# Experts in turn from four groups, a matmul branch for experts of at most 32 tokens, and the adding back moved

## The chip, the cores and the metric

The kernel runs on one core of one Trainium2 chip. The metric is the device time of one execution in microseconds (us), as the median over runs. The four compute engines have queues of their own: PE multiplies matrices (its weight loads are shown as PEld), DVE and ACT work on vectors and empty PSUM, POOL does little here, and SP issues most of the DMA transfers.

## The reference

The reference is a network of one batch of 512 tokens with 1024 columns in float32: an attention layer and a gated convolution layer, each followed by a SwiGLU layer, and then a block with windowed attention, an mLSTM and a mixture of experts. Only the last part, `hier_moe`, is touched:

- A router picks for every token one of 4 groups, and in that group the two best of 8 experts; so there are 32 experts and 1024 choices.
- Every expert e computes `(silu(x @ w_gate[e]) * (x @ w_up[e])) @ w_down[e]` for its tokens, with gate and up of 1024 x 512 and down of 512 x 1024.
- The result is multiplied by the token's weight and added to the token's row.

With the reference's inputs the router gives the experts these numbers of tokens, counted by running the reference's router (experts 0 to 31, eight to a group): 65 46 63 47 45 47 78 67 | 26 9 30 13 26 46 32 22 | 18 33 22 32 9 48 26 10 | 20 17 20 27 15 15 14 36. So 20 experts have at most 32 tokens, and three have more than 64: experts 0, 6 and 7.

## The kernel before

The layers ahead of the experts stream their weights through PE as products of split parts (`mm3`, lines 127 to 131) and take the first 1660 us. They stay as they are. The experts follow in one loop over e from 0 to 31 (lines 1545 to 1576), with the last one written out behind it. PE's instructions keep the order in which they are written (`manual_schedule`).

The work of an expert is done on 64 slots, the first 64 of its tokens. `place` (L1298) gives each choice its place among the tokens of its expert; a one-hot matrix of tokens by slots gathers the columns of the tokens (`gather`, L1395, for four experts at a time). In the order of PE one turn of the loop is:

- `turned` (L1440, tile htp): the hidden rows of expert e - 1 are transposed; ACT copies them to hT (L1442).
- `hidden` (L1431 and L1432, tile gu): gate and up of expert e. For each of 8 blocks of 128 rows there are two matmuls with 64 slots as the stationary part and 512 columns of weights moving; up's outputs go to one half of the partitions, gate's to the other. After the fourth and the eighth block `add_back_four` (L1467, tile cmb) puts in four matmuls that bring the outputs of expert e - 2 back to the rows of the tokens, and DVE adds each to X (L1469).
- `down` (L1452, tile y): the products of expert e - 1 with its down weights, for 4 blocks of 128 hidden columns, the two halves of the output columns side by side. ACT and DVE split and weight the outputs (L1457, L1459).
- An If on `any2` (L1562): if expert e or e - 1 has more than 64 tokens, the second 64 slots are worked on in `late_hidden` and `late_out`. PE, ACT and DVE read the count and branch.
- `gather` of a part of the next group (L1395), and `slot_weights` (L1421, tile otp), which transposes the weighted one-hot matrix into oT for the adding back; DVE takes the slots' weights from it (L1423).

The weights come in 192 pieces of 1 MB, six to an expert: gate, up, gate, up (halves of the rows), down, down. A ring of 14 buffers holds them, and `load_pieces` (L1188) issues them on SP's queue in order of use, each when its buffer comes free. In turn e the six pieces up to number 6e + 17 are asked for: their buffers are the ones of gate and up of expert e and of down of expert e - 1, so they come free when the If of turn e is over.

PSUM tiles come from two rings of four banks: "g" holds gu and y, "m" holds cmb, gat, otp and htp in the order in which they are written.

Of the kernel before, what the change touches and what calls it, by code (L numbers as in the profile page):

```python
# [9 lines left out]
F32 = mybir.dt.float32  # L10
# [11 lines left out]
P = 128  # L22
T = 512
# [18 lines left out]
def blocks_kernel(ctx: ExitStack, tc: tile.TileContext, a, out):  # L42
# [71 lines left out]
    def weave(*streams):  # L114
        """Emit the parts of several streams evenly: each is (generator, number of its parts)."""
# [11 lines left out]
    def mm3(ps, ah, al, bh, bl, start, stop):  # L127
        """ps += (ah + al)^T (bh + bl)"""
# [4 lines left out]
    def rsqrt(dst, src, n, eps, scale=1.0):  # L133
        """dst = 1 / sqrt(scale * src + eps) over [P, n], by three steps of Newton's; each turns the sign"""
# [4 lines left out]
    def newton(dst, h, n):  # L139
        """dst = 1 / sqrt(2 h)"""  # L140
# [13 lines left out]
    # -------------------------------------------------------------- constants  # L154
# [5 lines left out]
    def load_xt(t):  # L160
        """a token tile of x, columns on partitions, where its rows go later"""
# [9 lines left out]
    def to_T_half(xt, src, t, g):  # L171
        """512 columns (half g) of token tile t into the transposed pair."""
# [10 lines left out]
    # per-channel vectors, channels on partitions  # L183
# [23 lines left out]
    # relative position bias of every offset, the largest first, from which rows that start one  # L207
    # element further from row to row give the Toeplitz tile of a head, its columns turned round
# [15 lines left out]
    class Norm:  # L224
        """X = layer_norm(ALPHA X + m), tile after tile; the residual also gives the sums of the rows"""
# [30 lines left out]
    def rms_half(t, hh, ss, scr):  # L256
        """half of the mean of the squares of 512 columns' share"""
# [3 lines left out]
    def rms_scale(ss, eps):  # L261
        """1 / rms of a token tile from the two shares of half the mean square"""
# [7 lines left out]
    def out_parts(nk):  # L270
        """k ranges of an output projection for each half of the columns"""
# [8 lines left out]
    def out_half0(kh, kl, nk, fin, first=None):  # L280
        """The first 512 columns of k^T w for all tokens, token-major, k chunk after k chunk."""
# [45 lines left out]
    def proj_tm(xt, *evacs):  # L327
        """The next chunks' 256 columns token-major: evac(t, psum [128 tokens, 256])."""
# [10 lines left out]
    # ================================================ layer 0: diff attention  # L339
# [23 lines left out]
    with tc.tile_pool(name="att", bufs=2, side="right", reuse_waits="tile") as ap_, \  # L363
# [5 lines left out]
        def rotary(x):  # L369
            """rotate the first 16 of every 64 columns of x [P, NT, 256]"""  # L370
# [45 lines left out]
        def head_scores(u):  # L416
            """softmax difference of one head and query tile; one reciprocal row sum is left out"""
# [67 lines left out]
            # token tiles of a head that are normed together after the last of them  # L485
# [68 lines left out]
    # =============================================================== swiglu  # L554
# [3 lines left out]
    def proj_T(xt, evac, nk=KD):  # L558
        """The next chunk's 256 columns as rows: evac(i, psum [128 columns, tokens])."""
# [9 lines left out]
    def proj_T_first(xt, *evacs):  # L569
        """The same for the next two chunks, the first half of the tokens before the second."""  # L570
# [50 lines left out]
    # ================================================= layer 1: gated conv  # L621
# [51 lines left out]
    # ==================================================== second block, norm 1  # L673
# [21 lines left out]
    # gate rows: forward ig 0-3, backward ig 32-35, forward fg 64-67, backward fg 96-99  # L695
# [30 lines left out]
    def norm1_gain():  # L726
        """the gain of norm 1, which the weights behind it take up"""
# [6 lines left out]
    # ------------------------------------------- windowed attention, mLSTM  # L734
# [26 lines left out]
    # both parts of the 64 channels of a head one below the other, and the other way round  # L761
# [4 lines left out]
    def head_norm(x, n):  # L766
        """x [P, NT, n * 64] over its rms per 64 columns"""
        v = x.rearrange("p t (h e) -> p t h e", e=64)
        ss = small.tile([P, NT, n], F32, tag="hss", name="hss", bufs=1)
# [5 lines left out]
        rs = small.tile([P, NT, n], F32, tag="hrs", name="hrs", bufs=1)  # L775
# [18 lines left out]
    def proj_qk_m():  # L794
        """conv and twice the silu of the mLSTM queries and keys, channels on partitions"""
# [35 lines left out]
    def window_attn():  # L831
# [20 lines left out]
        def queries(i):  # L852
            """the two parts of two heads"""
# [20 lines left out]
    def window_scores(u):  # L874
        """softmax numerators of two heads of one query tile"""
# [48 lines left out]
    def branch_T(y, scales=None):  # L924
        """token-major y [P, NT, 512] into the transposed pair yT"""
# [24 lines left out]
    def proj_o():  # L950
        """sigmoid of the output gate"""
# [173 lines left out]
    def merge(i, out_cb):  # L1125
        """twice sigmoid(mg + b) * (y w) for one branch, rows are output columns"""
# [20 lines left out]
    # ------------------------------------------------------ merge, output  # L1147
# [34 lines left out]
    def load_pieces(end):  # L1182
        """the pieces up to the given number, those of an expert after those of the one before"""
        for n in range(sum(len(got) for got in pieces.values()), min(end, 6 * E_)):
# [3 lines left out]
            nc.sync.dma_start(p, a[key][0, e][hh * rows * P:(hh + 1) * rows * P]  # L1188
# [8 lines left out]
    iota65 = rt.tile([P, SLOTS], F32, tag="iota65", name="iota65")  # L1197
    nc.gpsimd.iota(iota65, [[1, SLOTS]], base=SLOTS + 1, channel_multiplier=0, allow_small_or_imprecise_dtypes=True)
# [450 lines left out]
```

## Time and profile before

| | us |
|---|---|
| three runs | 2274.31, 2275.84, 2276.46 |
| median | 2275.84 |
| span of the profiled execution | 2276.5 |
| PE busy in the span | 2173.3 (95%) |
| first to last gate/up matmul of the experts, start | 1664.46 to 2254.4 |

The page gives no time of the profiled execution beside its span; the span lies 0.04 us above the longest of the three runs. Times in the rows are counted from the span's start. A row of the timeline tells when an instruction began, how long it was in flight, its engine and line, and in brackets how long the engine had been idle before it and what ended the idle time. Matmuls overlap: one that is in flight for 0.59 us may be followed by the next after 0.43 us, so PE's pace is read from starts.

### The profile page before, as it was taken

Reading aid. Unit: us, or ns where it says so; the run is one execution under the profiler, and the core shown is the slowest. Engines: PE = TensorE matmul, PEld = TensorE weight load, DVE = VectorE, ACT = ScalarE, POOL = GpSimd, SP = SyncE. Lnnn points to the kernel's source line nnn. Section 1 sums busy time; section 2 is a strip of 40 time slices with the busy share of each in tenths; the row PEclk is TensorE's granted clock in tenths of the full one; section 3 lists DMA queues with packets and bytes.
Section 4 is the critical chain, followed back from the end, with each engine's and each line's share of the span. In section 5 each row is a group of like instructions: output and inputs, shape, how many; then the busy total and the mean of one; then the engine's idle time right before and its main releaser. Section 6 shows DMA issues by size and latency. Waiting matters only on the chain. (4 is left out here: it accounts for less than half of the span.)

```text
span 2276.5 us, 28917 instructions
## 1 busy us (share of the span) xinstructions
PE 2173.3 (95%) x11411; PEld 1623.8 (71%) x11412; DVE 1210.0 (53%) x2535; ACT 748.8 (33%) x1452; POOL 103.5 (5%) x90
## 2 busy tenths in 40 slices
PE   7999999999999999999997899999989989999997
PEld 7998788888888888888887788788844434444432
DVE  3788743332274463333237985774536445555555
ACT  3667533222132233232125454443322121212121
POOL 1000000000000000000012212121000000000000
PEclk9999999999999999999998999999999999999998
DMA  6210242232323223222232211323558849999994
GB/s 209 72 61 20 75 130 93 94 106 78 111 93 109 95 93 110 94 93 93 88 98 79 74 45 49 84 75 106 210 185 320 321 161 337 391 383 388 386 385 161
DMA packets 205290, 350.24 MB, mean 154 GB/s; under 512 B 8180, under 2 KB 101610, under 8 KB 205120
## 3 DMA queue, kind: packets, MB, share of 16 engines
q1 hardware_dynamic: 200784, 335.80, 42.2%
q0 software_dynamic: 3760, 11.09, 1.6%
q8 instruction: 112, 1.84, 0.3%
q10 hardware_dynamic: 576, 1.05, 0.1%
q14 instruction: 58, 0.48, 0.1%
HBM read 345.77 MB, written 2.13 MB: 153 GB/s over the span
## 5 line engine op out<-in xcount | busy, mean ns | idle before, releaser
L65 DVE TENSOR_TENSOR wlo<-raw,whi 128x1024 fp32r<-128x1024 f32 (+1 forms) x266 | 319.1, 1222 | 447.4 <-ACT whi L64 446.4
L130 PE MATMUL pT<-xl,whi 128*128 128x512 f32 (+1 forms) x1184 | 442.9, 374 | 1.3 <-DVE xl L65 1.3
L131 PE MATMUL pT<-xh,whi 128*128 128x512 f32 (+1 forms) x1184 | 443.1, 374 | 0.0
L129 PE MATMUL pT<-xh,wlo 128*128 128x512 f32 (+1 forms) x1184 | 442.5, 374 | 0.0
L64 ACT ACTIVATE whi<-raw 128x1024 fp32r<-128x1024 f32 (+1 forms) x266 | 258.1, 1005 | 345.4 <-PE po L131 169.2
L1431 PE MATMUL gu<-piece,xg 128*64 128x512 f32 x560 | 255.9, 601 | 4.8 <-DVEq L1580 2.7
L1432 PE MATMUL gu<-piece,xg 128*64 128x512 f32 x560 | 255.9, 601 | 0.0
L1469 DVE TENSOR_TENSOR X<-X,cmb 128x512 f32<-128x512 f32 x280 | 173.3, 683 | 152.3 <-PE cmb L1467 152.0
L130 PEld LDWEIGHTS pT<-xl,whi 128*128 128x128 f32 x1184 | 224.0, 189 | 40.2 <-DVE xl L65 1.7
L131 PEld LDWEIGHTS pT<-xh,whi 128*128 128x128 f32 x1184 | 223.8, 189 | 38.8
L129 PEld LDWEIGHTS pT<-xh,wlo 128*128 128x128 f32 x1184 | 223.8, 189 | 38.1
L129 PE MATMUL pq<-whi,xl 128*128 128x256 f32 x608 | 180.2, 296 | 14.1 <-ACT whi L64 12.6
L130 PE MATMUL pq<-wlo,xh 128*128 128x256 f32 x608 | 176.7, 291 | 7.8 <-DVE wlo L65 7.8
L131 PE MATMUL pq<-whi,xh 128*128 128x256 f32 x608 | 176.9, 291 | 0.0
L1431 PEld LDWEIGHTS gu<-piece,xg 128*64 128x64 f32 x560 | 71.7, 137 | 142.8 <-issue 135.0
L131 PE MATMUL po<-whi,hh 128*128 128x512 f32 x352 | 140.4, 399 | 0.0
L129 PE MATMUL po<-whi,hl 128*128 128x512 f32 x352 | 140.1, 398 | 0.0
L130 PE MATMUL po<-wlo,hh 128*128 128x512 f32 x352 | 140.1, 398 | 0.0
L1452 PE MATMUL y<-piece,hT 128*64 128x512 f32 x560 | 129.2, 604 | 2.1 <-ACT hT L1442 2.1
L129 PEld LDWEIGHTS pq<-whi,xl 128*128 128x128 f32 x608 | 120.2, 198 | 14.8 <-ACT whi L64 12.5
L130 PEld LDWEIGHTS pq<-wlo,xh 128*128 128x128 f32 x608 | 120.1, 198 | 8.8 <-DVE wlo L65 8.5
L131 PEld LDWEIGHTS pq<-whi,xh 128*128 128x128 f32 x608 | 120.0, 197 | 0.2
(402 smaller groups left out, 3078.4 us busy)
## 6 DMA issues: line engine op xcount, KB each, us to landing
piece<-in_w_expert_gate SPq DMA_DIRECT2D x64, 1024.0 KB, 7.7
piece<-in_w_expert_up SPq DMA_DIRECT2D x64, 1024.0 KB, 10.2
piece<-in_w_expert_down SPq DMA_DIRECT2D x64, 1024.0 KB, 14.3
raw<-in_ffn_w_gate SPq DMA_DIRECT2D x22, 1024.0 KB, 5.3
raw<-in_ffn_w_up SPq DMA_DIRECT2D x22, 1024.0 KB, 5.3
raw<-in_ffn_w_down SPq DMA_DIRECT2D x20, 1024.0 KB, 5.0
raw<-in_w_in SPq DMA_DIRECT2D x19, 1024.0 KB, 5.1
raw<-in_conv_w_in SPq DMA_DIRECT2D x12, 1024.0 KB, 5.1
```

Of the source, the lines that this page charges most:

```text
L64: act.activation(hi, src, AF.Copy)
L65: dve.tensor_tensor(out=lo, in0=src, in1=hi.bitcast(F32), op=ALU.subtract)
L129: pe.matmul(ps, al, bh, start=start, stop=False)
L130: pe.matmul(ps, ah, bl, start=False, stop=False)
L131: pe.matmul(ps, ah, bh, start=False, stop=stop)
L1431: pe.matmul(gu[rows], xs(k), pc_[2 + k // 4][:, k % 4, :], **st)
L1432: pe.matmul(gu[other], xs(k), pc_[k // 4][:, k % 4, :], **st)
L1452: pe.matmul(y[rows], hT[:, f, :], pc_[4 + f // 2][:, f % 2, c * 512:(c + 1) * 512], **st)
L1469: dve.tensor_tensor(out=sl, in0=sl, in1=ps, op=ALU.add)
```

## The change

The experts are numbered anew: `ORDER` takes one from each group in turn, and the weights, the router's expert numbers (`iotae`) and the loop over the remaining blocks follow it. In the new order the numbers of tokens are, from turn 0 to turn 31: 65 26 18 20 46 9 33 17 63 30 22 20 47 13 32 27 45 26 9 15 47 46 48 15 78 32 26 14 67 22 10 36.

`cnt` now holds the number of tokens of each expert, and `hidden` and `down` each read it on PE alone and branch. For more than 32 tokens the matmuls are those of before. For at most 32 tokens gate and up are done as four tiles of 32 columns at once, each on 32 slots and 256 columns of weights, after one bf16 matmul of zeros that starts the bank; and down as four tiles, two for the halves of the output columns times two for the halves of the hidden rows. To make this work, slots 32 to 63 of such an expert get the same tokens as slots 0 to 31 (`io`, `few`), so that adding back sums the two halves of down. The adding back of expert e - 2 is no longer inside `hidden`: four of its matmuls come before `hidden(e)` and four after it; in the last turn all eight of expert 30 come behind `hidden(31)`.

```diff
+    ORDER = [8 * (n % G_) + n // G_ for n in range(E_)]
...
-            nc.sync.dma_start(p, a[key][0, e][hh * rows * P:(hh + 1) * rows * P]
+            nc.sync.dma_start(p, a[key][0, ORDER[e]][hh * rows * P:(hh + 1) * rows * P]
...
-    pc = psum.tile([1, E_], F32, tag="m", name="pc")
+    pcs_ = psum.tile([P, E_], F32, tag="m", name="pc")
...
+    dve.tensor_scalar(out=few, in0=pcs_, scalar1=float(HALF), scalar2=None, op0=ALU.is_le)
...
+        dve.scalar_tensor_tensor(out=io[:, HALF:], in0=few[:, e:e + 1].to_broadcast([P, HALF]), scalar=-float(HALF),
+                                 in1=iota1[:, HALF:], op0=ALU.mult, op1=ALU.add)
...
+    def gate_up_few(gu, xs, pc_):
+        zero = ident[0:HALF].bitcast(BF16)[:, 2 * HALF:].unsqueeze(1)
+        pe.matmul(gu, zero[:, :, 0:P], zero[:, :, 0:P].to_broadcast([HALF, 4, P]), start=True, stop=False)
+        for k in range(KD):
+            st = dict(start=False, stop=k == KD - 1)
+            for q in range(4):
+                cs = slice(q % 2 * 256, q % 2 * 256 + 256)
+                pe.matmul(gu[quarter(q), cs], xs(k)[:, 0:HALF],
+                          pc_[(2 if q < 2 else 0) + k // 4][:, k % 4, cs], **st)
+
+    def few_tokens(e):
+        return nc.values_load(cnt[0:1, e:e + 1], engines=[ET.PE], min_val=0, max_val=2 * T,
+                              skip_runtime_bounds_check_because="a count of choices") <= HALF
...
+        gu = pbank("g", "gu")
+        with tc.If(few_tokens(e)) as c:
+            gate_up_few(gu, xs, pieces[e])
+        with c.Else():
+            gate_up_all(gu, xs, pieces[e], LOW)
+        activated(gu, s, LOW)
...
+    def down_few(y, hT, pc_):
+        for f in range(2):
+            st = dict(start=f == 0, stop=f == 1)
+            for q in range(4):
+                c, i = divmod(q, 2)
+                pe.matmul(y[quarter(q)], hT[:, 2 * i + f, quarter(i)],
+                          pc_[4 + i][:, f, c * 512:(c + 1) * 512], **st)
...
+            if e > 1:
+                add_back_four(e - 2, 0)
...
-            hidden(lambda k: xg[:, k, r * SLOTS:(r + 1) * SLOTS], pieces[e], ss[e], LOW, between)
+            hidden(e, lambda k: xg[:, k, r * SLOTS:(r + 1) * SLOTS], ss[e])
+            if e > 1:
+                add_back_four(e - 2, 1)
             if e > 0:
-                ys[e - 1] = down(hT, pieces[e - 1], ws[e - 1], "y")
+                ys[e - 1] = outputs(down(e - 1, hT), ws[e - 1], "y")
...
+        hidden(e, lambda k: xg[:, k, r * SLOTS:(r + 1) * SLOTS], ss[e])
...
+        add_back_four(e - 1, 0)
+        add_back_four(e - 1, 1)
+        yy = outputs(down(e, turned(ss[e], LOW)), sw, "y")
```

Beside this, the late slots of an expert are found with another DVE operation of the same size, two small tiles of the windowed attention (`hss`, `hrs`) move to another pool, and comments go.

## Rows read from the trace of the kernel before

**Rows 1.** The page: busy time, clock and DMA rate in 40 slices of 56.9 us.

```profile
PE 2173.3 (95%) x11411; PEld 1623.8 (71%) x11412; DVE 1210.0 (53%) x2535; ACT 748.8 (33%) x1452; POOL 103.5 (5%) x90
...
PEclk9999999999999999999998999999999999999998
...
GB/s 209 72 61 20 75 130 93 94 106 78 111 93 109 95 93 110 94 93 93 88 98 79 74 45 49 84 75 106 210 185 320 321 161 337 391 383 388 386 385 161
```

**Rows 2.** Stretches: busy us of PE, PEld, DVE, ACT, POOL; clock, DMA share, GB/s.

```profile
1711.00:1879.00 168.00, 156.28 (x764) 70.51 (x764) 86.97 (x155) 34.26 (x61) 0.00 (x0) 0.99 0.73 270
1993.00:2205.00 212.00, 205.63 (x1026) 91.40 (x1026) 122.29 (x224) 42.83 (x78) 0.00 (x0) 1.00 1.03 386
```

**Rows 3.** Timeline of PE in one turn (expert 18).

```profile
2025.56 0.64 PE L1431 MATMUL gu<-piece,xg 128*64 128x512 f32 x1
2025.57 0.64 PE L1432 MATMUL gu<-piece,xg 128*64 128x512 f32 x1
2026.04 0.59 PE L1431 MATMUL gu<-piece,xg 128*64 128x512 f32 x1
...
2029.14 1.19 PE L1467 MATMUL cmb<-y,oT 128*128 128x512 f32 x4
...
2030.27 0.64 PE L1431 MATMUL gu<-piece,xg 128*64 128x512 f32 x1
...
2034.98 3.65 PE L1452 MATMUL y<-piece,hT 128*64 128x512 f32 x16
...
2039.09 0.36 PE L1395 MATMUL gat<-oh,h2l 128*128 128x256 f32 x1 [0.46 <-PEq L1562]
...
2041.93 0.64 PE L1431 MATMUL gu<-piece,xg 128*64 128x512 f32 x1
```

**Rows 4.** Timeline: the first gate/up matmul of experts 0, 2, 6, 9, 20, 31.

```profile
1664.46 0.64 PE L1431 MATMUL gu<-piece,xg 128*64 128x512 f32 x1
...
1713.94 0.64 PE L1431 MATMUL gu<-piece,xg 128*64 128x512 f32 x1
...
1779.41 0.64 PE L1431 MATMUL gu<-piece,xg 128*64 128x512 f32 x1
...
1878.12 0.64 PE L1431 MATMUL gu<-piece,xg 128*64 128x512 f32 x1
...
2058.29 0.64 PE L1431 MATMUL gu<-piece,xg 128*64 128x512 f32 x1
...
2244.94 0.81 PE L1431 MATMUL gu<-piece,xg 128*64 128x512 f32 x1 [2.71 <-DVEq L1580]
```

**Rows 5.** SP issues by tile up to the first 24 pieces, and the next issue.

```profile
piece<-in_w_expert_gate SPq DMA_DIRECT2D x8, 1024.0 KB, 5.9
...
1727.15 0.37 SPq L1188 DMA_DIRECT2D piece<-in_w_expert_gate  x1
```

**Rows 6.** One stretch, columns as in rows 2.

```profile
1723.00:1724.00 1.00, 1.00 (x6) 0.34 (x6) 1.00 (x3) 0.00 (x0) 0.00 (x0) 1.00 0.02 8
```

**Rows 7.** Timeline of DVE, the same turn.

```profile
2023.89 1.53 DVE L1459 SCALAR_TENSOR_TENSOR y<-y,sw 64x512 fp32r<-64x512 f32 x2
...
2025.96 0.69 DVE L1423 TENSOR_REDUCE sw<-otp 128x1 f32<-128x512 f32 x1 [0.53 <-ACT oT L1422]
```

**Rows 8.** Lines of the If and of its load: ns min/median/max, first and last start.

```profile
L1562 PEldq COMPARE_BRANCH  x31: 70/330/433, 1667.7 to 2230.0; - x31
...
L1508 PEldq TENSOR_LOAD <-any x31: 297/302/493, 1667.1 to 2229.6; - x31
```

**Rows 9.** Waits of PE: us in total, times, longest.

```profile
PE gat L1395 <- PEq L1562: 10.6, 23, 0.6
PE cmb L1467 <- DVE y L1459: 10.0, 7, 2.3
...
PE gat L1395 <- PEq L1566: 1.0, 1, 1.0
```

**Rows 10.** Timeline of DVE ahead of the first turn.

```profile
1665.71 0.16 DVE L1352 CAST cnt<-ex 1x32 int32<-1x32 f32 x1
```

More of the change, by code (lines that the diff above doesn't have):

```diff
@@ L1210, in blocks_kernel @@
     nc.gpsimd.iota(iota, [[1, SLOTS]], base=0, channel_multiplier=0, allow_small_or_imprecise_dtypes=True)
+    iotae = r1.tile([P, E_], F32, tag="iotae", name="iotae")
+    nc.gpsimd.iota(iotae, [[1, E_ // G_], [E_ // G_, G_]], base=0, channel_multiplier=0,
+                   allow_small_or_imprecise_dtypes=True)
     sel = r1.tile([P, NT, E_], BF16, tag="sel", name="sel")
@@ L1351, in blocks_kernel @@
         dve.scalar_tensor_tensor(out=ex, in0=pc, scalar=float(SLOTS * m), in1=ex, op0=ALU.is_gt, op1=ALU.add)
[L1352 to L1356 removed]
+    dve.tensor_copy(cnt, pc)
+    dve.tensor_copy(any2[:, 0:1], ex[:, 0:1])
+    dve.tensor_tensor(out=any2[:, 1:E_], in0=ex[:, 1:E_], in1=ex[:, 0:E_ - 1], op=ALU.add)
     ge = r1.tile([P, NT, G_], F32, tag="ge", name="ge")
@@ L1423, in slot_weights, with quarter, gate_up_all @@
         dve.reduce_max(out=w, in_=ps, axis=AX.X)
-    def hidden(xs, pc_, s, rows, between=lambda k: None):
-        gu = pbank("g", "gu")
+    def quarter(i):
+        return slice(i * HALF, (i + 1) * HALF)
+    def gate_up_all(gu, xs, pc_, rows):
         other = HIGH if rows == LOW else LOW
@@ L1432, in hidden, with activated @@
             pe.matmul(gu[other], xs(k), pc_[k // 4][:, k % 4, :], **st)
-            between(k)
+    def gate_up_few(gu, xs, pc_):
[10 more added lines that the diff above has]
+                              skip_runtime_bounds_check_because="a count of choices") <= HALF
+    def activated(gu, s, rows):
+        other = HIGH if rows == LOW else LOW
         act.activation(s[rows], gu[other], AF.Silu)
         dve.tensor_tensor(out=s[rows], in0=s[rows], in1=gu[rows], op=ALU.mult)
+    def hidden(e, xs, s):
+        gu = pbank("g", "gu")
[4 more added lines that the diff above has]
+        activated(gu, s, LOW)
     def turned(s, rows):
@@ L1452, in down, with outputs @@
                 pe.matmul(y[rows], hT[:, f, :], pc_[4 + f // 2][:, f % 2, c * 512:(c + 1) * 512], **st)
-        between()
+    def down_few(y, hT, pc_):
[5 more added lines that the diff above has]
+                          pc_[4 + i][:, f, c * 512:(c + 1) * 512], **st)
+    def down(e, hT):
+        y = pbank("g", "y")
+        with tc.If(few_tokens(e)) as c:
+            down_few(y, hT, pieces[e])
+        with c.Else():
+            down_all(y, hT, pieces[e])
+        return y
+    def outputs(y, w, tag):
         yt = x1.tile([P, 2, T], F32R, tag=tag, name="y")
@@ L1469, in add_back, with add_back_four @@
         dve.tensor_tensor(out=sl, in0=sl, in1=ps, op=ALU.add)
-    def add_back_four(e, k):
-        if k % 4 == 3:
-            for i in range(k - 3, k + 1):
-                add_back(oTs[e], ys[e], i)
+    def add_back_four(e, j):
+        for i in range(4 * j, 4 * j + 4):
+            add_back(oTs[e], ys[e], i)
     def late_slots(e):
         oh = x1.tile([P, NT, SLOTS], F32R, tag="oh1", name="oh1")
-        dve.tensor_tensor(out=oh, in0=posm[:, :, e:e + 1].to_broadcast([P, NT, SLOTS]),
-                                in1=iota65.unsqueeze(1).to_broadcast([P, NT, SLOTS]), op=ALU.is_equal)
+        dve.scalar_tensor_tensor(out=oh, in0=iota1.unsqueeze(1).to_broadcast([P, NT, SLOTS]), scalar=float(SLOTS),
+                                 in1=posm[:, :, e:e + 1].to_broadcast([P, NT, SLOTS]),
+                                 op0=ALU.add, op1=ALU.is_equal)
         return oh
@@ L1499, in late_hidden, with if_some @@
         act.activation(xg, ps, AF.Copy)
-        hidden(lambda k: xg[:, k, :], pc_, s, HIGH)
+        gu = pbank("g", "gu")
+        gate_up_all(gu, lambda k: xg[:, k, :], pc_, HIGH)
+        activated(gu, s, HIGH)
     def late_out(s, pc_):
-        yy = down(turned(s, HIGH), pc_, late_w, "late")
+        y = pbank("g", "y")
+        down_all(y, turned(s, HIGH), pc_)
+        yy = outputs(y, late_w, "late")
         for i in (*range(0, 2 * NT, 2), *range(1, 2 * NT, 2)):
             add_back(late_o, yy, i)
-    def if_some(count):
+    def if_some(count, over=0):
         return tc.If(nc.values_load(
-            count, engines=[ET.PE, ET.Activation, ET.DVE], min_val=0, max_val=2 * T // SLOTS,
-            skip_runtime_bounds_check_because="counts of blocks among all the tokens") > 0)
+            count, engines=[ET.PE, ET.Activation, ET.DVE], min_val=0, max_val=2 * T,
+            skip_runtime_bounds_check_because="counts among all the tokens") > over)
     def remaining_blocks():
@@ L1576, in blocks_kernel @@
             slot_weights(ow, oTs[e], ws[e])
-        between(3)
-        ys[e - 1] = down(hT, pieces[e - 1], ws[e - 1], "y", lambda: between(7))
-        with if_some(cnt[0:1, e - 1:e]):
+        y = down(e - 1, hT)
+        add_back_four(e - 2, 1)
+        ys[e - 1] = outputs(y, ws[e - 1], "y")
+        with if_some(cnt[0:1, e - 1:e], SLOTS):
             late_out(ss[e - 1], pieces[e - 1])
@@ L1584, in blocks_kernel @@
         ow = expert_weights(e)
-        hidden(lambda k: xg[:, k, r * SLOTS:(r + 1) * SLOTS], pieces[e], ss[e], LOW,
-               lambda k: add_back_four(e - 1, k))
+        hidden(e, lambda k: xg[:, k, r * SLOTS:(r + 1) * SLOTS], ss[e])
         oT = x2.tile([P, T], F32R, tag="oT", name="oT")
@@ L1589, in blocks_kernel @@
         slot_weights(ow, oT, sw)
-        yy = down(turned(ss[e], LOW), pieces[e], sw, "y")
-        with if_some(cnt[0:1, e:e + 1]):
+        add_back_four(e - 1, 0)
+        add_back_four(e - 1, 1)
+        yy = outputs(down(e, turned(ss[e], LOW)), sw, "y")
+        with if_some(cnt[0:1, e:e + 1], SLOTS):
             late_hidden(late, wtok[:, :, e:e + 1], pieces[e], ss[e])
```

40 lines of the change are left out of this document (18 added, 22 removed).

## The prediction

> **What bounds the kernel now.** I read the page's slices first: PE is busy 95% of the span at a granted clock of 1.0 (the 2.4 GHz level) nearly throughout, and in slices 34 to 39 of the 40 the DMA rate climbs to 383 to 391 GB/s, which it reaches nowhere earlier [rows 1]. The change touches only the experts, from 1664.46 on [rows 4], so I cut that part into stretches. From 1711 to 1879 DMA moves 270 GB/s, from 1993 to 2205 it moves 386 at a share of 1.03, and PE is busy 93% and 97% [rows 2]. Both engines are nearly full in the second stretch. Which one holds the other? In a steady turn nothing on PE waits for a piece: one turn lasts 2041.93 - 2025.56 = 16.37 us, with one gap of 0.46 us at the skipped If [rows 3]. So PE is the bound, and DMA stands close behind it: six pieces of 1024 KB (1.0486 MB) at the 391 GB/s of the densest slice [rows 1, 5] take 6 x 2.68 = 16.1 us. A turn can lose only 0.3 us before DMA takes over, unless DMA has been idle elsewhere. It has: experts 6 and 7 have second slots, and from hidden(6) to hidden(9) go 98.71 us [rows 4] instead of 3 x 16.37 = 49.1. That is 24.8 us for each such expert, in which the ring of 14 pieces fills and DMA stops.
>
> **The change, part by part.**
>
> *Gate/up of few tokens.* Now two halves, 2025.56 to 2029.14 and 2030.27 to the next cmb, 3.58 each: 7.16 us [rows 3]. A pass of 512 float32 columns for two tiles lasts 0.43 (L1431 and L1432 start 0.01 apart; the first pass takes 0.48, and 3.58 = 0.48 + 7 x 0.43 + the change to cmb), and there are 16 passes. With four tiles of 256 columns side by side a pass should take half, 0.215: 16 x 0.215 = 3.44, plus the matmul of zeros (a quarter of the four cmb, which start 1.13 before the next gu: about 0.25) and two changes of the tile's shape (0.05 to 0.1 each, from 0.48 against 0.43). I take 3.9, so 3.26 less. Bounds: all side by side and nothing beside, 3.44; two at a time, 16 x 0.43 + 0.4 = 7.3, no gain; one at a time, about 14. I take the first, since the two tiles of now share a pass without any loss [rows 3].
>
> *Down of few tokens.* 4 passes of 0.43 instead of 8: 1.72 less of the 3.6 us from 2034.98 on; bounds 0 and 1.8. Together s = 4.98 us for each of 20 experts.
>
> The Trainium skill, "TensorE: Matmul & The Clock Gate", section "Measured speedup vs the span model", gives 3.07 times for four row tiles and 2.38 times for three column tiles, not 4 and 3. By it a pass of four would take 1.3 times the ideal, s would be 3.55, and the sum below 2257; no row here has four tiles, and the two of now lose nothing.
>
> *Adding back ahead of hidden.* The eight matmuls stay (four take 1.13), but the first four now come right behind htp. They need y of expert e - 2, which DVE finishes at 2023.89 + 1.53 = 2025.42, just before the place where they would start (2025.56); and the third needs the bank of otp, which DVE frees with the reduce at 2025.96 + 0.69 = 2026.65, against 2025.56 + 0.5 [rows 3, 7]. So PE waits some 0.6 us, 0.7 with the rest; behind it queue gate/up, and so DVE's and ACT's work on them. Bounds: -0.1 (one change of shape fewer) and 2.3, the longest wait of a cmb for y now [rows 9].
>
> *Two Ifs more in each turn.* On PE a count is loaded (0.30) and compared (0.07 to 0.43) [rows 8]. Where matmuls are queued ahead this is hidden; what shows now is the 0.46 us at the end of the skipped If. Behind the new waits stand all later matmuls of PE, since it is one queue. Bounds: 0, and 2 x 0.97, the idle where two branches follow each other [rows 9]; I take 0.8 for both, near the 0.46 of one. So o = 0.7 + 0.8 = 1.5 us more in each turn, bounds -0.1 and 4.2.
>
> *The first branch.* hidden(0) now must know its count; the cast ends at 1665.87 [rows 10], hidden(0) starts at 1664.46 [rows 4]. With load and branch that is 2 to 2.5 us late, once; expert 1 has few tokens and gives about as much back before the second burst of pieces. I take 0, bounds -1 and 3.
>
> *At nothing:* the order, `iotae`, `few`, the count over 128 columns and the other operation for late slots, and one short operation on `io` per turn: DVE is busy 122.3 of 212 us [rows 2]; without that cover the last would cost 0.2 us a turn, which lies in o's bounds. SP issues the same 192 transfers at the same place of the turn. In the last turn the eight add-backs behind hidden(31) wait for DVE's adds, but DVE then has the product for htp earlier: 0, bounds -3 and 3.
>
> **The sum.** Two limits. PE alone: hidden(2) starts at 1713.94, and the 18 turns to hidden(20) hold 13 few experts: 1714 + 18 x (16.37 + 1.5) - 13 x 4.98 = 1971. DMA: by 1723 the first 24 pieces (eight of each of three weights) are in and the queue is empty, and expert 4's first piece is issued only at 1727.15, when the If of turn 2 is over [rows 5, 6]. In the new kernel that turn has few tokens: 1727.15 - 4.98 + 1.5 = 1723.7. The piece lands 5.9 later, the median of the gate pieces to there [rows 5], and from then on the short turns ask for pieces sooner than DMA brings them. hidden(20) needs 99 more: 1729.6 + 99 x 2.68 = 1995. So DMA is the later one, by 24 us, and holds PE until about hidden(20). From there PE has the long experts (47 46 48 . 78 . . . 67) and leads: in the old kernel hidden(20) to the end is 2276.5 - 2058.29 = 218.2 [rows 4]; add 11 turns x 1.5 = 16.5, and two experts with second slots, 2 x 24.8 = 49.6; take off 6 x 3.26 + 7 x 1.72 = 31.6. 1995 + 218.2 + 16.5 + 49.6 - 31.6 = **2247.7**. In this the third long expert stays at the start as before, and the times of experts 6 and 7 (49.6) only change place; the gain comes from DMA running in the stretch where it moved 270 GB/s. If PE is the later one throughout, the same terms give 2276.5 + 29 o - 19.4 s; at o = 1.5 and s = 4.98 that is 2223, below the other. The span is 0.7 above the median of the runs, so I predict a median of 2247.
>
> DMA's rate counts 100 pieces: at 2.60 us (403 GB/s) the sum is 8 lower, at 2.75 7 higher. In the stretch where PE waits for pieces, its clock may fall: after the 2.71 us idle at 2244.94 the next start comes after 0.60 instead of 0.48 [rows 3, 4]. PE has 24 us of room there, so I take 0, bound 6 us more.
>
> **The rivals.**
>
> 1. *The overhead eats the saving* (o of 2.5 to 4, or s near 3). For it: every new wait is on PE's single queue. Against: the one If of now costs 0.46. At o = 3.2: 2276.5 + 92.8 - 96.6 = 2273. 2264 to 2281.
> 2. *Slower: the four tiles do not run four at a time.* Place: the few branch of 20 turns; price 4.98 a turn of saving that fails, with o paid in all turns: 2276.5 + 43.5 = 2320. It decides from s below 2.25 (29 x 1.5 / 19.4). For it: no row shows four; against: two share a pass fully.
> 3. *Slower: branches stall.* Each taken arm jumps over the other, and PE waits for code. Price from the wait at hidden(31), behind a jump over a loop that all engines pass: 2.7 us [rows 4]; twice a turn gives o = 6.1 and 2276.5 + 177 - 97 = 2357. Against: 23 waits at the skipped If, whose body is larger, sum to 10.6 us, 0.6 at most [rows 9]. The Trainium skill, "Runtime: NRT & Kernel Launch", section "Instruction fetch mechanics", says that a taken branch out of the fetched window stalls for the fetch; those 23 skips show none.
> 4. *Faster still:* DMA at 2.60 and o near 0: 1722.2 + 5.9 + 99 x 2.60 + 218.2 + 49.6 - 31.6 = 2222. For it: counts may be loaded far ahead. 2214 to 2232.
>
> **How the numbers follow.** The forecast (2232 to 2264, its own range) has a chance of 0.55, rival 1 0.15, rival 2 0.12, rival 3 0.08, rival 4 0.10. About 0.2% can be told from no change, 2271 to 2280. Faster: 0.55 + 0.10 and 0.09 of rival 1, 0.74; within: 0.06; slower: 0.12 + 0.08 = 0.20. The range reaches from the upper part of rival 4 to beyond rival 1: 2224 to 2290; outside are 0.04 below and 0.18 above.
>
> **What would show it.** Right: gate/up of a few expert takes about 3.9 us with starts in fours; DMA at 380 GB/s or more from about 1723 to 2050; PE idle before gate/up, ended by a piece, in turns 8 to 20; no such waits after; long turns at the new places 24, 25, 28, 29. Wrong: passes of four 0.43 apart (rival 2); PE idle behind branches of over 1 us (rival 3); PE never waiting for a piece although few experts are short (then o is larger than I took, or s smaller); DMA pieces landing faster than 2.6 us apart.

## The result: slower by 0.9%, and the profile after

The changed kernel takes 2297.86 us (median of 4 runs, 2292.95 to 2302.80) against 2276.15 for the kernel before on the same chip: a ratio of 1.0091, 95% interval 1.0065 to 1.0116. I had predicted 2247. The profiled execution is the shortest of the four, 2292.95 us, with a span of 2291.2.

The page of the changed kernel, beside [rows 1]: fewer PE us, but the clock falls off at the end, and the DMA rate is high earlier and no longer at 385 in slices 36 to 39.

```profile
PE 2126.8 (93%) x12071; PEld 1624.0 (71%) x12072; DVE 1213.7 (53%) x2567; ACT 752.8 (33%) x1453; POOL 104.5 (5%) x91
...
PEclk9999999999999999999998999999999999999887
...
GB/s 222 61 56 20 118 102 92 92 108 76 111 99 104 92 107 96 92 93 109 92 73 99 42 38 67 83 97 184 156 203 382 369 362 370 379 358 322 265 247 79
```

The experts begin at 1654.83 in this execution and at 1664.46 in that of before [rows 4]. No product of the layers ahead was changed, and in the runs below the experts begin anywhere between 1656.9 and 1668.9, so I compare the experts' part alone. First before, then after (columns as in [rows 2]: stretch, its length, busy us by engine, granted clock, DMA share, GB/s):

```profile
1664.46:2276.50 612.04, 570.04 (x2761) 250.14 (x2760) 328.45 (x595) 122.25 (x216) 0.00 (x0) 0.98 0.84 313
```

```profile
1654.83:2291.20 636.37, 531.54 (x3420) 257.30 (x3420) 332.02 (x621) 125.30 (x215) 0.00 (x0) 0.91 0.81 301
1711.00:1879.00 168.00, 145.50 (x1041) 73.15 (x1042) 98.64 (x186) 34.18 (x60) 0.00 (x0) 0.94 1.00 373
...
1993.00:2205.00 212.00, 183.45 (x1097) 86.59 (x1098) 107.19 (x199) 41.47 (x72) 0.00 (x0) 0.92 0.87 322
```

PE's idle time, length less busy, rises from 42.0 to 104.8 us. The granted clock falls from 0.98 to 0.91: by the trace's clock records PE stands at its lower level (1.2 GHz) for 21 us before and 113 after. Count a busy us at that level as half, and PE's work at full clock is 562.6 before and 480.0 after. So the work fell by 82.6 us; idle time took back 62.8 and the lower clock 44.0 (7.5 before, 51.5 after). The sum is +24.3 us, 636.4 - 612.0. The change did its work and lost more than all of it in pauses and in the lower clock behind them.

Two turns show the two kinds of pause. PE's timeline of the turn of expert 10, 22 tokens (columns as in [rows 3]):

```profile
1841.04 0.38 PE L1450 MATMUL gu<-ident 32*128 32x512 bf16 x1
1841.35 3.66 PE L1455 MATMUL gu<-piece,xg 128*32 128x256 f32 x64
1844.94 1.20 PE L1524 MATMUL cmb<-y,oT 128*128 128x512 f32 x4
1846.08 1.48 PE L1497 MATMUL y<-piece,hT 128*32 128x512 f32 x9
1847.79 1.06 PE L1497 MATMUL y<-piece,hT 128*32 128x512 f32 x7 [0.24 <-issue]
1849.32 0.36 PE L1404 MATMUL gat<-oh,h2l 128*128 128x256 f32 x1 [0.47 <-PEq L1623]
...
1850.22 0.28 PE L1404 MATMUL gat<-oh,h2h 128*128 128x256 f32 x1
1854.22 0.37 PE L1404 MATMUL gat<-oh,h2l 128*128 128x256 f32 x1 [3.72 <-issue]
...
1855.89 1.06 PE L1433 MATMUL otp<-ident,ow 128*128 128x128 f32 x4
```

Gate/up is 1841.04 to 1844.94, 3.90 us instead of 7.16 [rows 3]. But in the middle of the gather, whose operands have been there for long, PE stops for 3.72 us, and the DMA queues of 1850.5 to 1854.2 show an instruction packet, that is a block of program code, beside the pieces (packets, MB, share):

```profile
q8 instruction: 1, 0.02, 1.7%
```

What follows is read from the clock column of these stretches:

```profile
1850.50:1854.00 3.50, 0.00 (x1) 0.00 (x0) 2.33 (x6) 0.00 (x0) 0.00 (x0) 1.00 1.02 393
1854.00:1857.50 3.50, 3.28 (x17) 2.83 (x16) 0.00 (x0) 1.12 (x2) 0.00 (x0) 0.51 1.05 388
1857.50:1861.00 3.50, 3.30 (x34) 1.64 (x37) 2.97 (x5) 0.46 (x2) 0.00 (x0) 1.00 1.06 389
```

After the pause PE runs 3.4 us at half clock: the same gather matmuls start 0.21 apart instead of 0.12. The other kind of pause, in the turn of expert 5, first DVE, then PE:

```profile
1766.69 0.59 DVE L1424 TENSOR_SCALAR ow<-io,posm,wtok 128x128 f32<-128x128 f32 x2
1767.31 1.51 DVE L1516 SCALAR_TENSOR_TENSOR y<-y,sw 64x512 fp32r<-64x512 f32 x2
1768.84 0.60 DVE L1424 TENSOR_SCALAR ow<-io,posm,wtok 128x128 f32<-128x128 f32 x2
```

```profile
1768.03 0.38 PE L1433 MATMUL otp<-ident,ow 128*128 128x128 f32 x2
1769.24 0.58 PE L1433 MATMUL otp<-ident,ow 128*128 128x128 f32 x2 [0.83 <-DVE ow L1424]
```

DVE makes half of ow, then y, which nobody needs yet, then the rest of ow, and PE waits for that. The list of PE's waits in the experts' part (us, times, longest):

```profile
PE otp L1433 <- DVE ow L1424: 31.7, 29, 3.6
PE gat L1404 <- PEq L1623: 19.7, 22, 2.5
PE cmb L1524 <- DVE y L1516: 9.0, 4, 2.3
PE gat L1404 <- issue: 6.2, 2, 3.7
...
PE gu L1444 <- DVE ex L1385: 2.5, 1, 2.5
```

The first of these is new, the second was 10.6 with no wait over 0.6 [rows 9]. Before, the first was:

```profile
PE otp L1421 <- DVE ow L1412: 2.4, 3, 0.9
```

No wait for a piece of weights is in the list of after.

### The profile page after: what moved, and what is told of

It reads as the page before. It is cut to its first block, busy times and chain, and to the rows that moved or that the text cites. A ratio compares the mean times of both kernels' runs of the same rounds, so it can differ in the third digit from the quotient of the medians.

```text
span 2291.2 us, 30420 instructions
## 1 busy us (share of the span) xinstructions
PE 2126.8 (93%) x12071; PEld 1624.0 (71%) x12072; DVE 1213.7 (53%) x2567; ACT 752.8 (33%) x1453; POOL 104.5 (5%) x91
## 5 line engine op out<-in xcount | busy, mean ns | idle before, releaser
L129 PEld LDWEIGHTS pq<-whi,xl 128*128 128x128 f32 x608 | 118.6, 195 | 13.7 <-ACT whi L64 10.7
L1444 PE MATMUL gu<-piece,xg 128*64 128x512 f32 x240 | 116.3, 641 | 10.5 <-PEq L1459 3.1
L1445 PE MATMUL gu<-piece,xg 128*64 128x512 f32 x240 | 116.3, 642 | 0.0
L1524 PE MATMUL cmb<-y,oT 128*128 128x512 f32 x256 | 96.3, 474 | 10.9 <-issue 2.4
L88 POOL TENSOR_TENSOR raw<-raw,vecs 128x2048 f32<-128x2048 f32 (+1 forms) x20 | 72.1, 3605 | 554.3 <-DMA raw<-in_w_in 471.1
```

The lines of the kernel that those rows point to most:

```text
L88: nc.gpsimd.tensor_tensor(out=raw, in0=raw, in1=gain().unsqueeze(2).to_broadcast([P, kt, cols]), op=ALU.mult)
L129: pe.matmul(ps, al, bh, start=start, stop=False)
L1444: pe.matmul(gu[rows], xs(k), pc_[2 + k // 4][:, k % 4, :], **st)
L1445: pe.matmul(gu[other], xs(k), pc_[k // 4][:, k % 4, :], **st)
L1524: pe.matmul(ps, oT[:, t * P:(t + 1) * P], yy[c], start=True, stop=True)
```

## The experiments

Theory A: what the narrow tiles save goes into short pauses of PE that the tests bring (by the order in which DVE gets its instructions, and by code loading, which is PE waiting for its own instructions to arrive) and into the lower clock behind the pauses. Rivals: B, the tests' own time; C, the moved additions delay ow; D, the narrow tiles themselves lower the clock; E, the new order of experts. All numbers in one table; idle, lower clock and work are made as above, from the first gate/up matmul to the end. They are us of one execution each (e4's took 6 us more than its median, e10's 7 us less); "lower clock" is the time at the lower level, of which the busy part costs half. The runs stand on several chips, and each ratio is to the kernel before on the same chip (medians 2275.53 to 2279.93), so I compare ratios.

| run | median us | ratio to before, 95% | idle | lower clock | work at full clock |
|---|---|---|---|---|---|
| before | 2276.15 | | 42.0 | 21 | 562.6 |
| changed | 2297.86 | 1.0091 (1.0065 to 1.0116) | 104.8 | 113 | 480.0 |
| e1 order only | 2286.00 | 1.0042 (1.0027 to 1.0056) | 45.7 | 31 | 562.8 |
| e2 + additions moved | 2306.00 | 1.0124 (1.0106 to 1.0142) | 52.8 | 45 | 571.4 |
| e3 + tests, never true | 2377.00 | 1.0424 (1.0405 to 1.0444) | 90.3 | 96 | 578.3 |
| e4 narrow, fixed choice | 2256.09 | 0.9898 (0.9882 to 0.9915) | 88.8 | 47 | 484.9 |
| e5 changed, ow first | 2273.15 | 0.9976 (0.9960 to 0.9992) | 89.1 | 102 | 473.9 |
| e6 e5, gate/up only | 2271.71 | 0.9978 (0.9961 to 0.9996) | 72.4 | 69 | 510.3 |
| e7 turn reordered | 2402.77 | 1.0556 (1.0519 to 1.0592) | 183.0 | 202 | 468.5 |
| e8 e7, fixed choice | 2264.58 | 0.9941 (0.9923 to 0.9959) | 86.6 | 65 | 482.1 |
| e9 changed, gap filled | 2279.10 | 1.0022 (1.0005 to 1.0039) | 76.4 | 81 | 507.1 |
| e10 e7, orders by hand | 2285.01 | 1.0057 (1.0030 to 1.0085) | 100.0 | 95 | 478.5 |
| e11 e5, orders by hand | 2282.55 | 1.0030 (1.0008 to 1.0053) | 107.5 | 113 | 469.0 |
| e12 e11, one-hot early | 2259.40 | 0.9923 (0.9894 to 0.9951) | 89.3 | 82 | 472.4 |
| e13 e5, longer code | 2321.32 | 1.0205 (1.0160 to 1.0251) | 131.0 | 126 | 470.8 |
| e14 e3, ow first | 2337.83 | 1.0268 (1.0239 to 1.0296) | 73.1 | 72 | 572.1 |
| e15 e10, one-hot early | 2268.84 | 0.9971 (0.9953 to 0.9989) | 85.9 | 91 | 480.2 |
| e16 e12, gate/up only | 2262.96 | 0.9948 (0.9933 to 0.9963) | 68.7 | 55 | 509.5 |

### The change taken apart: e1 to e4

e1 and e2 keep no test and no narrow tiles; e1 has the additions inside gate/up again. e3 has the tests, but never true. e4 fixes the choice in the program.

```diff
# e1, e2, e4: no test
-        with tc.If(few_tokens(e)) as c:
-            gate_up_few(gu, xs, pieces[e])
-        with c.Else():
-            gate_up_all(gu, xs, pieces[e], LOW)
+        if e in FEW_EXPERTS:        # e1, e2: []; e4: the 20 experts of this input
+            gate_up_few(gu, xs, pieces[e], between)
+        else:
+            gate_up_all(gu, xs, pieces[e], LOW, between)
...
# e3 (and few compared with 0, as in e1 and e2)
-                              skip_runtime_bounds_check_because="a count of choices") <= HALF
+                              skip_runtime_bounds_check_because="a count of choices") <= 0
```

> Order of the experts (and the few extra vector operations) alone: every expert on 64 rows, no test of the count on TensorE, four additions back after each half of gate/up as in the kernel before. Theory A (short TensorE gaps made by the tests, by code loading and by the late weights ow cost once as idle time and once more as half clock; the order costs nothing): like the kernel before, 2276 us within 6. Rival E (the order of the experts or the moved piece loads cost the time): 2285 us or more.

> The same with the additions back moved out of gate/up to before and after it; still no test and no narrow tiles. Theory A: small loss, 2276 to 2290 us, since the wide down product (3.4 us) hides ow behind it better than the narrow one. Rival C (the moved additions delay the vector engine's ow, and that is the whole loss): 2295 to 2310 us.

> The whole change with its two tests per expert in place, but the condition is count <= 0, which is never true: all experts take the wide branch. Theory A: the tests and the code loading cost 20 to 35 us of idle time and up to as much of half clock above the run with moved additions: 2300 to 2335 us. Theory B (tests and code loading alone, no clock): 2300 to 2315. Rival D (the narrow tiles themselves lower the clock): within 8 us of the run with moved additions.

> Narrow tiles for the same 19 experts, but the choice is fixed in the program for this input: no count is read by TensorE and no branch is taken, and the other arm's code is not there. Additions back moved as in the changed kernel. Theory A: about 35 us of idle time and some 20 of half clock go: 2243 us, range 2225 to 2260. Theory B: 2298 less 22 to 35 of stalls: 2263 to 2276. Rival C (ow on the vector engine alone): 2290 or more. Rival D: half clock stays over 100 us and the time is 2263 or more.

The four ratios split the change. Order: +0.42%, some 10 us. I had it at nothing within 6 us, and the 2286.00 lies in rival E's range: E is right for this much. The trace shows 7.5 us of it: 3.7 us more of idle time, 3.0 of them in waits for ow (5.4 us in three), and 10 us more at the lower clock, worth 3.7. Why the clock fell there stays open. Moved additions: 1.0124 / 1.0042, +19 us; C's 2295 to 2310 was the nearer figure, but not its reason: the waits for ow are 5.5 us in three, as in e1. What grew are waits for sw (5.3), PE's work (8.6) and the lower clock (14 us). Narrow tiles without a test: 0.9898 / 1.0124, -51 us. Tests with narrow tiles: 1.0091 / 0.9898, +44 us. The four steps add up to the whole by the way they are made, so their sum is no test of them. With tests that are never true they cost more still, 1.0424 / 1.0124, 68 us, though not one narrow tile runs; that was above every theory's figure. D falls with it, and with e4, where the narrow tiles run and the lower clock is 47 us against e2's 45. The tests bring the waits for ow; e2's list, then e3's:

```profile
PE otp L1433 <- DVE ow L1424: 5.5, 3, 2.7
```

```profile
PE otp L1433 <- DVE ow L1424: 34.6, 33, 3.6
PE gat L1404 <- PEq L1623: 10.6, 23, 0.5
```

The reason stands on DVE. The program fixes the order on PE alone; on DVE and ACT a planner sets it when the program is built. Without tests (e2) it puts all of ow ahead of y, as the lines below show; with them, as in the turn of expert 5 above, y comes into the middle of it. (Tests are not the only thing that does this: in e4, without tests, y cuts into ow in some turns too, and PE waits 11.8 us for ow, in six waits.) In e2:

```profile
1739.21 1.11 DVE L1424 TENSOR_SCALAR ow<-io,posm,wtok 128x128 f32<-128x128 f32 x4
1740.35 1.53 DVE L1520 SCALAR_TENSOR_TENSOR y<-y,sw 64x512 fp32r<-64x512 f32 x2
```

In e4 the work is as low as in the changed kernel, 484.9, and yet only 51 of the 86.5 us below e2 reach the end. Its waits and its DMA say where the rest is:

```profile
PE gat L1404 <- ACTq L1627: 24.7, 16, 1.5
...
PE gu L1456 <- DMA piece<-in_w_expert_up: 10.5, 6, 3.0
...
PE gu L1444 <- DMA piece<-in_w_expert_up: 3.2, 4, 1.6
```

```profile
1711.00:1879.00 168.00, 150.49 (x1118) 75.45 (x1116) 109.37 (x207) 38.01 (x67) 0.00 (x0) 0.99 1.02 383
1879.00:1993.00 114.00, 92.24 (x767) 47.63 (x766) 68.62 (x129) 24.68 (x45) 0.00 (x0) 1.00 1.04 393
```

Here PE does wait for pieces, at a DMA share above 1.0: the limit that the prediction put at hidden(20) exists, and the kernels without tests, e4 and e8, reach it; of those with tests only e6, e12 and e16 wait for pieces, 4 to 7 us each. And 16 times PE waits 1.54 us at the If for second slots, until ACT, which has y's two copies ahead of it, has passed that If too.

### The order on DVE and the turn: e5 to e8

```diff
# e5
-                ys[e - 1] = outputs(down(e - 1, hT), ws[e - 1], "y")
+                y = down(e - 1, hT)
             with if_some(any2[0:1, e:e + 1]):
...
             ow = expert_weights(e)
+            if e > 0:
+                ys[e - 1] = outputs(y, ws[e - 1], "y")
# e6: e5, and
-        with tc.If(few_tokens(e)) as c:
-            down_few(y, hT, pieces[e])
-        with c.Else():
-            down_all(y, hT, pieces[e])
+        down_all(y, hT, pieces[e])
# e7, e8 (e8 with e4's fixed choice): PE's turn; ow made at the end of the turn before
+  htp, gather, add_back_four(e - 2, 0), add_back_four(e - 2, 1), otp, gate/up, down, If for second slots, outputs
```

> The changed kernel with one edit: the vector and scalar engines' outputs of the narrow or wide down product are written in the program behind the branch for second blocks and behind ow, so that ow no longer stands behind y on the vector engine. Theory A (with the tests in the program, ow ends up behind y, TensorE's otp waits for it about 1 us a turn, and these gaps also bring half clock): idle falls by about 30 us and the half clock's cost by 10 to 25, so 2245 to 2262 us. Theory B (the tests and code loading alone): 2286 to 2293. Rival F (the wait only moves to y at the next additions back): 2288 to 2298.

> As the run before, but only gate/up has a test and narrow tiles; down is always wide and untested: 19 x 1.72 = 33 us of work come back, and half of the tests go. Theory A: the remaining tests cost some 30 to 40 us in all, so half of that against 33: within 10 us of the run before. Theory B (each test costs over 1 us of idle time whatever the vector engine does): 10 to 20 us below the run before.

> The changed kernel, general as it is (tests kept), with the turn in another order on TensorE: turned hidden rows, gather, first four additions back, second four, slot weights, gate/up, down, branch for second blocks; ow made at the end of the turn before, y's outputs behind the branch. Theory A: the 20 us of the moved additions and the ow waits both go: 2228 to 2250 us, with waits for pieces appearing. Theory B: 2270 to 2290.

> The same order, with the choice of narrow or wide fixed in the program for this input and no tests. Theory A: TensorE gets ahead of the transfers, which become the bound: 2210 to 2240 us with over 25 us of waits for pieces. Rival: if the transfers do not bind, 2190 to 2205.

e5 takes the waits for ow from 31.7 to 8.5 us and the time down by 25 us (1.1% by the ratios), over half of the 44 us of the tests; that part came through the order on DVE (and on ACT, whose copies of y move with it). It misses its expectation by 11 us: idle time falls by 15.7 instead of 30, and the lower clock only from 113 to 102. The pauses behind the If stay; some 27 us at the lower clock begin in such a pause or within 4 us of its end, against 17 in the changed kernel.

```profile
PE gat L1404 <- PEq L1623: 20.1, 22, 2.7
...
PE otp L1433 <- DVE ow L1424: 8.5, 5, 3.6
```

e6 gives back 36 us of saving (473.9 to 510.3) and loses nothing, as expected. e7 is the clearest miss. A turn that is better on paper is 5.6% slower, because with tests the planner now puts s behind the If, ow and y on DVE:

```profile
1911.25 1.11 DVE L1424 TENSOR_SCALAR ow<-io,posm,wtok 128x128 f32<-128x128 f32 x4
1912.39 1.51 DVE L1516 SCALAR_TENSOR_TENSOR y<-y,sw 64x512 fp32r<-64x512 f32 x2
1913.93 0.68 DVE L1465 TENSOR_TENSOR s<-s,gu 64x512 f32<-64x512 f32 x1
```

```profile
PE htp L1480 <- DVE s L1465: 140.0, 32, 6.8
```

e8, the same turn without tests, has one such wait of 3.7 us. Its 2264.58 is above e4 and outside its expected range: the waits for y are 21.2 us there, against 10.4 in e4, and those for pieces 15.6 instead of the 25 or more that I expected.

### The clock by itself: e9

```diff
+            fill = pbank("m", "fill")
+            for i in range(4):
+                pe.matmul(fill, h2h[:, 0, 0:P], h2h[:, 0, 0:512], start=True, stop=True)
             slot_weights(ow, oTs[e], ws[e])
```

> The changed kernel with four more products of 128x512 (whose results nobody reads, into a bank of its own) ahead of the slot weights in every turn, about 0.93 us of TensorE work each turn and 29 us in all, where TensorE waits for ow (33.4 us in 30 waits). Theory A (gaps bring half clock, which costs as much again): half clock falls from 113 us to 60 to 85, and the time falls 5 to 20 us although work was added: 2278 to 2293. Rival G (the half clock has nothing to do with these waits): 2298 to 2310, half clock within 10 us of 113.

27 us more of work and a kernel that is 0.7% faster (1.0022 against 1.0091). Waits for ow fall to 10.7 us and idle time by 28.4 in all, as much as the work that was added; what is won is the lower clock, which falls from 113 to 81 us, 15 us by its cost. Rival G is out: pauses of PE bring the lower clock, and it costs time of its own.

```profile
PE otp L1433 <- DVE ow L1424: 10.7, 7, 1.7
```

```profile
1656.93:2277.00 620.07, 543.64 (x3544) 271.73 (x3544) 331.83 (x621) 125.90 (x215) 0.00 (x0) 0.93 0.83 308
```

### Orders by hand: e10, e11, e12, e15

```diff
-    with tc.manual_schedule(engines={ET.PE}):
+    with tc.manual_schedule(engines={ET.PE, ET.Activation, ET.DVE}):   # e11: e5's turn; e10: e7's, with ow behind the additions and otp behind gate/up
# e12 (from e11) and e15 (from e10)
-                if r == 0:
-                    one_hot(g + 1)
+                if e == 0:
+                    one_hot(1)
                 gather(*groups[g + 1], GRP * SLOTS, 2 * r, 2 * r + 2)
+                if r == GRP - 1 and g + 2 < E_ // GRP:
+                    one_hot(g + 2)
```

> The changed kernel, tests kept, in the reordered turn but with the vector and the scalar engine's order also written out by hand: y's outputs, the eight additions, ow, second-block slots, the gated hidden rows s, the slot weights; on TensorE gather, eight additions back, gate/up, slot weights, down, branch. Theory A (the waits of TensorE come from the order on the vector engine, which the planner sets badly around a test): no wait for s (140 us in the reordered run before), ow under 3 us, and 2240 to 2260 us. Theory B (the tests themselves): 2275 or more.

> The changed kernel in its own turn, outputs behind the branch and ow as in the run with ow first, but with the vector and the scalar engine's order written out by hand. Theory A: like the run with ow first (2273) less what is left of waits for ow and sw, 2255 to 2272. Rival: the second four additions back stand ahead of the branch on the vector engine and TensorE waits for its end: 2280 to 2300.

> As the run in the changed kernel's own turn with the orders by hand, with the one-hot of a group made at the end of the group before, where TensorE does not wait for it (37.6 us of waits in that run, 7 of them). Theory A (the waits are the vector engine's order): those waits go and some half clock with them, 2235 to 2260 us. Rival (the tests and code loading are what is left and the waits only move): 2268 or more.

> As the reordered turn with the orders by hand (2285), with the one-hot of a group made a turn earlier (16.4 us of waits for it before). Theory A: 2255 to 2272 us. Rival: 2278 or more.

e10 removes the 140 us of waits for s, so these were the planner's order; it and e11 miss, in good part because the one-hot now stands in DVE's order right ahead of the gather that needs it (16.4 and 37.6 us of waits). e11's 2282.55 lies in its rival's range, but not by the wait that the rival named. With the one-hot a turn earlier e15 is some 20 us below e10, in its expected range, and e12 is 0.77% faster than the kernel before, with both tests in it: the fastest kernel here that chooses at run time. It ends at the upper end of its expected range. What it still waits for is, first of all, the If:

```profile
PE gat L1404 <- PEq L1626: 18.8, 14, 4.8
PE gat L1404 <- DVEq L1626: 8.8, 9, 1.0
```

### Is the rest code loading? e13, e14, e16

```diff
# e13: e5, and inside the If for second slots
+                with if_some(cnt[0:1, e:e + 1], 2 * T - 1):
+                    more = pbank("m", "more")
+                    for i in range(64):
+                        pe.matmul(more, h2h[:, 0, 0:P], h2h[:, 0, 0:512], start=True, stop=True)
# e14: e3 with e5's edit; e16: e12 with e6's edit
```

> The run with ow first, and behind the branch for second blocks' arms one more test inside that branch with 64 products (128x512) that is never true for any count: nothing more is computed, but each turn's program has some 128 to 256 more TensorE instructions to skip. Theory L (what is left is the loading of instructions after a skip): more pauses of 2 to 4 us in the gather, instruction packets from 133 to over 150, and 2300 to 2360 us. Rival (the tests' own waits): 2273 within 8.

> The run with tests that are never true (2377, all experts wide) with the outputs and ow ordered as in the run with ow first. Theory A (of the 71 us that the tests cost there, the wait for ow and the half clock that it brings are the most): 2310 to 2335 us. Rival (the tests' own cost): 2355 or more.

> The fastest kernel with tests so far (orders by hand, one-hot a turn earlier: 2259) without down's test: down always wide, 20 x 1.72 = 34 us of work come back, and one of two tests a turn goes with its arms. Theory L (loading of skipped instructions and the half clock it brings are what is left of the tests' price): 18.8 + 5.0 us of pauses and some 20 us of half clock go for the most part, so within 6 us of 2259. Rival (down's test costs next to nothing): 2280 to 2293.

e13 executes none of the added products, and still the waits at the exit of the skipped If grow from e5's 20.1 to 65.1 us and the time by about 50, in the range of theory L. Its waits and its instruction queue, which the page has at 133 packets for the changed kernel and at 134 for e5:

```profile
PE gat L1404 <- PEq L1623: 65.1, 24, 5.9
```

```profile
q8 instruction: 150, 2.46, 0.4%
```

The 16 packets more than in e5 say only that the longer code is brought in though none of it runs. What ties the pauses to the loading is their time. By the trace's DMA records the changed kernel has ten pauses of 1.4 to 3.7 us between 1829 and 2003 for which no other engine is named, and each of them ends 1.4 to 2.1 us after an instruction packet has landed; only 65 such packets come in the 636 us. In e13, 21 of the 22 pauses over 1.3 us in the gather end in the same way. The pieces of weights, which move at the same time, are a rival: these ten pauses fall where the DMA share of the 20 us before is 0.82 or more. But e4 and e6 move 393 GB/s from 1879 to 1993 without such a pause at the If, and e13 has two at shares of 0.72 and 0.73. Whether pieces make a pause longer was not tested.

e14, all experts wide, has no code pause at the If, as before the change:

```profile
PE gat L1404 <- PEq L1623: 10.6, 23, 0.5
```

So the tests alone don't starve PE of instructions; the tests with narrow tiles do. A reason, argued and not shown: the narrow arm has 65 gate/up passes in 3.9 us where the wide one has 32 in 7.2, so PE uses up its instructions nearly four times as fast and then jumps. e14 is some 36 us below e3 by the ratios, as A had it (3 us above its range), but still 33 us above e2: some 1 us a turn, 20 us of it idle time and 13 the lower clock, is left of the tests' price with the order mended. e16 has one test instead of two, and down always wide. The waits at the If are 10.3 us and 0.5 at most, the lower clock 55 us instead of 82, and 37 us more of work cost only 4 to 6 us of time. e6, made from e5 in the same way, has no such pause at the If either (10.7 us in 23 waits, 0.6 at most); both have one of 1.84 us elsewhere, at the additions behind gate/up. Whether the test that went or the slower pace of the wide down does it, these runs don't separate.

```profile
PE gat L1404 <- PEq L1623: 10.3, 22, 0.5
```

The Trainium skill, "Runtime: NRT & Kernel Launch", section "Instruction fetch mechanics", has a taken branch out of the fetched window wait for a fetch; the pauses of 1.4 to 5.9 us here agree. It counts fetching as mostly hidden in straight code; e4, narrow but with one jump a turn, has no such pause.

## Why the prediction was wrong

**Right:** gate/up of few tokens, predicted 3.9, takes 3.90 in 12 of its 20 turns (longer in the others, where the lower clock or a pause falls into it); down, predicted 1.9, goes from 1715.87 to 1717.79 in the turn of expert 2, 1.92. s is (7.16 - 3.90) + (3.65 - 1.92) = 4.99, predicted 4.98; rival 2 (tiles not side by side) is out. The first branch waits 2.5 us (2 to 2.5 predicted). DMA as the next limit: e4 shows it, though without tests.

**Right by luck:** the moved additions at 0.7 a turn. e1 to e2 is 19 us, 0.6 a turn; but the waits that I had added up, for y and for the bank that the reduce of sw frees, grow by 0.8 and 5.3 us over the whole stretch, and the rest is work that grew by 8.6 and the lower clock.

**The step that failed is o**, "0.8 for both" of the two Ifs and "1.5 us more in each turn". In the prediction's own formula, 2276.5 + 29 o - 19.4 s, the experts' part should have fallen by 19.4 x 4.99 = 96.8 us beside o, and it grew by 24.3; so o took 121.1 us, 4.2 in each of the formula's 29 turns or 3.9 in each of 31. Over 31 turns that is 2.0 of idle time (62.8), 1.4 of lower clock (44.0) and the rest, 0.5, of work that did not go. I had bounded o at 4.2, so it came out at the end of the bound. Rival 1 named the case: at its own upper o of 4 the formula gives 2296, but I closed its range at 2281 and gave it 0.15. Since PE never got ahead of DMA, the 24 us of room that hid the overhead up to hidden(20) were not there either.

Inside o three things were priced wrongly. First, I looked at what a test costs on PE, which it is read on; the largest part of the new idle time came from DVE, which reads no count: the order that the planner makes around a test put y into ow (29 of the 62.8 us; e5: 25 us of time; e7: 140 us of waits for s). Secondly, rival 3 argued from the 23 skips of before that code is there in time [rows 9]. Those skips came at the pace of wide passes. With narrow passes the changed kernel has the ten pauses of above, 23 us together: not two in each turn, as rival 3 had it, but not none. Thirdly, the clock: "24 us of room there, so I take 0, bound 6" for 44 us.

**Also off:** the order at nothing (10 us); and the 0.7 us taken off for the step from span to median, since the span of an execution here is 1.7 us below its time (2291.2 and 2292.95). A part of what the narrow tiles save would also have been lost without any test: 35 of e4's 86.5 us, of which the prediction had the waits for pieces, but not ACT's 24.7 us at the If. Of the kernels with both tests, only those with another order on DVE are faster than before (e5, e12, e15).

## What to carry to other kernels

A test on one engine is paid on all of them: look at the order that the planner gives the other engines on both sides of it, and write it out if it matters. When work gets shorter, price a pause twice, once as idle time and once as the lower clock that may follow, and ask whether instructions still arrive in time at the new pace. Saving on a path with several narrow margins gives back less than its size: 86 us of work saved were worth 51 without a test (e2 to e4), and 91 us were worth 8 with two (e2 to the changed kernel).

## What the runs showed of the hardware

- Four column tiles of 32, each with 256 float32 columns, run side by side with hardly a loss: 64 passes in 3.59 us, where half the 0.43 us of two tiles of 512 columns would make 3.44. The Trainium skill's "TensorE: Matmul & The Clock Gate", section "Measured speedup vs the span model", has less than the ideal for three column tiles and for four row tiles; for the four column tiles of this trace that does not hold, with s at 4.99 us where its factor gave an estimate of 3.55.
- TensorE fell to 1.2 GHz behind pauses: 3.72 us idle, then 3.4 us at 0.51. Adding 27 us of unread products made a kernel 0.7% faster. Not every pause does it: in e4 neither fourteen of 1.54 us before 2010 nor waits for pieces of up to 3.0 us around 1900 and 1982 were followed by a fall (1.00 in 1879 to 1993), and in the changed kernel only four of the ten code pauses were. What sets them apart stays open.
- Instructions that are skipped cost time: 64 products behind a test that is never true, 45 us of waits over 31 turns. That these waits are the loading is shown by their growth with the length of the skipped code and by the packets: each of the changed kernel's ten pauses ends 1.4 to 2.1 us after one has landed. What that time is made of, no run shows.
